# Seven products instead of eight in five units of a pair of merge gates: one more unit in each of three pairs

## The chip, the core and the metric

The kernel runs on one core of a Trainium2 chip. The metric is the device time of one execution in microseconds (us). A core has a matrix engine (TensorE, PE in the profile, with its weight loads as PEld), a vector engine (DVE), a scalar engine (ACT), GpSimd (POOL) and a sync engine (SP) that issues most of the DMA transfers. Each engine takes its instructions in order from a queue of its own and waits at an instruction until what it needs is there.

## The reference

One decoder layer on 256 tokens with a width of 2048, in float32:

```
h = rmsnorm(x, norm_mix_g)
u = h @ w_in                       # split into ten parts
ya = b * causal_dwconv3(c * xa) * silu(za)
yb = rmsnorm(hgrn2(silu(q), f, iv)) * silu(og)
m = sigmoid(ga) * (ya @ w_a) + sigmoid(gb) * (yb @ w_b)
x = x + m @ w_o
x = x + sigmoid(rmsnorm(x) @ w_ple_gate) * (p @ w_ple_proj)
out = rmsnorm(x, final_norm_g)
```

The merge gates ga and gb are the last two parts of u, 2048 columns each. They are what the change is about: `h @ w_in` for 2 x 2048 columns, over a depth of 2048.

## The kernel before

**Products.** Matrices are multiplied in blocks of 128 tokens by 512 columns with a depth of 128. Each float32 operand is split into a high and a low part in a format that TensorE takes at full speed, and a product is three matmuls, high by high, high by low and low by high (`triple`, L1012 to L1014). The token side (`state["hT"]`, xh and xl in the profile) is split once. The weights come from memory all the way through and are split on the fly: ACT copies the high part (whi, L149) and DVE subtracts it from the source to get the low part (wlo, L150). Both are in `cut` and `split`; there are four pairs of whi and wlo buffers.

**Order of the work.** The list `items` holds one entry for each 256 rows of depth by 512 columns of weights. The main loop goes through it and issues, for the item at `pos`: first the combining of the weights of the item at `pos + 2` where that one is of kind S (below), then the split of the item at `pos + 3` (LEAD is 3), then the products of the item itself, then loads further ahead, and then one step of each epilogue that is under way (`advance`). The planner orders TensorE's queue and the DMA queue by its own forecast of when operands are ready. From the gates on, `pinned` fixes the queues of ACT and DVE to the written order.

**Pairs of gates.** Column group j of ga and of gb (512 columns each) form a pair. Pair 0 is multiplied plainly. In pairs 1 to 3 the depth of 2048 falls into eight units of 256 rows. A unit is a product of two by two blocks: two blocks of 128 tokens, two of 128 rows of depth, two of 512 columns. `SEVEN` names the units that are done with seven products instead of eight, by sums and differences of blocks (kind S); the others are kind C, two items of four products. Before, units 0, 2, 4 and 6 are of kind S, so the order is S C C S C C S C C S C C. An S unit needs

- its raw weights, both column groups, in one sraw tile (two buffers);
- the split of the first column group (whi and wlo, L149 and L150), as for any item;
- from `combine_weights` (L164): the split of the block raw[3] (bhi and blo, one buffer), the differences L169, L170 and L171 on DVE in place in sraw, and the split of the four results in two steps (thi and tlo, three buffers);
- sums of token blocks (shi and slo), made once for all pairs by `token_sums` (L715).

`unit_products` (L1039) issues its products in the order of `names_of` (L1029): P1, c00, c10 (into banks s), P5, P7, P6, c01 (into banks g), with the weights whi, whi, bhi, then the halves of thi. P1 and the two c's take the first split, c10 bhi, P5 and P7 the first thi, P6 and c01 the second.

**Banks.** Four accumulation banks are tagged g and four s. A pair takes all eight, g for P6, c01, P5 and P7. Between two pairs the products A (ya by w_a) and B (yb by w_b), four items each, take two banks g each. They are read by DVE: `ep_a` multiplies A into ga (L748), `ep_bb` multiplies B into gb (L760) and adds the two (L764). `ep_bb` is issued at the end of the loop step of the last B item.

**Token sums.** `token_sums` is a generator that moves on by one `yield` at each item after the last one of ga in pair 0. There are 16 items from there to the first S unit. It makes the sums of units 0 and 2, then those of units 4 and 6: each time after four idle steps, the float32 tokens (L726), then in the next step four additions and subtractions (L738) and the split (L740 and L741).

**Memory.** The pool const lasts for the whole kernel, tmp1 until the end of the branches. When `second_part` closes tmp1, the pool st (sraw, bhi, blo, thi, tlo, and the token sums) and tmp2 take its room. The scan's constant `carry` and the masks `near_m` and `full_m` lie in const, and are used only while tmp1 is open.

Of the kernel before, what the change touches and what calls it, by code (L numbers as in the profile page):

```python
# [9 lines left out]
F32 = mybir.dt.float32  # L10
F32R = mybir.dt.float32r
AF = mybir.ActivationFunctionType
ALU = mybir.AluOpType
PSUM = bass.MemoryType.PSUM

P = 128
T = 256
# [11 lines left out]
LB_MAX = 1.0 - 1e-6  # L29
SCAN = 64  # L30
LEVELS = [32, 16, 8, 4]
SEVEN = [(), (0, 2, 4, 6), (0, 2, 4, 6), (0, 2, 4, 6)]
NARROW, Q = len(LEVELS), 32


# [11 lines left out]
def hybrid_kernel(ctx, tc, xT, x, pT, prm, gfin, masks, w_in, w_a, w_b, w_o, w_pg, w_pp, out):  # L47
    nc = tc.nc

    const = ctx.enter_context(tc.tile_pool(name="const", bufs=1))  # L50
# [7 lines left out]
    pools, closers = {}, {}  # L58
# [13 lines left out]
    state = {"tmp": "tmp1"}  # L72
# [3 lines left out]
    def nm(s):  # L76
        uid[0] += 1
        return f"{s}_{uid[0]}"

    def t4(tag="t4", bufs=None):  # L80
        bufs = bufs or {"tmp1": 8, "tmp2": 3, "tmp3": 5}[state["tmp"]]
        return pools[state["tmp"]].tile([P, 1024], F32, tag=tag, bufs=bufs, name=nm(tag))

    def bank(tag):
        return ps.tile([P, CW], F32, tag=tag, bufs=4, name=nm(tag))

    def sc(n, tag="sc", bufs=12):
        return small.tile([P, n], F32, tag=tag, bufs=bufs, name=nm(tag))
# [16 lines left out]
    for gi, (kind, j, w, g, op) in enumerate(groups):  # L105
        if kind == "gb" and SEVEN[j]:
            continue
        for c in range(w.shape[2]):
            it = {"gi": gi, "kind": kind, "j": j, "c": c, "last": c == w.shape[2] - 1}
            if kind != "ga" or not SEVEN[j]:  # L110
                key = ("PP", j // 2) if kind == "PP" else (gi, c // 2)
                items.append(dict(it, w=(w, g, c), raw=key, slot=(j if kind == "PP" else c) % 2))
            elif c in SEVEN[j]:
                items.append(dict(it, kind="S", w=(w, g, c), raw=(gi, c)))
# [6 lines left out]
    def raw_of(pos):  # L121
        it = items[pos]
        if it["raw"] not in loaded:
            if it["kind"] == "S":
                t = pools["st"].tile([P, 2, 2 * CW], F32, tag="sraw", bufs=2, name=nm("sraw"))
            else:
                t = wp.tile([P, 2, 2 * CW], F32, tag="raw", bufs=3, name=nm("raw"))
            loaded[it["raw"]] = t
        return loaded[it["raw"]]
# [15 lines left out]
    def pair_of(pool, n, tags=("whi", "wlo"), width=2 * CW):  # L145
        return tuple(pool.tile([P, width], F32R, tag=tag, bufs=n, name=nm(tag)) for tag in tags)

    def cut(hi, lo, src):
        a = nc.scalar.activation(out=hi, in_=src, func=AF.Copy)  # L149
        v = nc.vector.tensor_tensor(out=lo, in0=src, in1=hi.bitcast(F32), op=ALU.subtract)  # L150
        state["splits"] = (a.ins, v.ins)
# [12 lines left out]
    def combine_weights(pos):  # L164
        st = pools["st"]
        raw = raw_of(pos).rearrange("p n (k c) -> p (n k) c", k=2)
        b22 = pair_of(st, 1, ("bhi", "blo"), CW)
        cut(b22[0], b22[1], raw[:, 3, :])
        nc.vector.tensor_tensor(out=raw[:, 0::2], in0=raw[:, 2:4], in1=raw[:, 0::2], op=ALU.subtract)  # L169
        nc.vector.tensor_tensor(out=raw[:, 3], in0=raw[:, 3], in1=raw[:, 0], op=ALU.subtract)  # L170
        nc.vector.tensor_tensor(out=raw[:, 1], in0=raw[:, 1], in1=raw[:, 3], op=ALU.subtract)  # L171
        ts = []
        for i in range(2):
            hi, lo = pair_of(st, 3, ("thi", "tlo"))
            cut(*(v.rearrange("p (n c) -> p n c", n=2) for v in (hi, lo)), raw[:, i::2])
            ts += [(hi[:, n * CW : (n + 1) * CW], lo[:, n * CW : (n + 1) * CW]) for n in range(2)]
        sums[pos] = (b22, *ts)
# [51 lines left out]
    nc.gpsimd.memset(mhalf, -0.5)  # L229

    nc.scalar.activation(out=sc(8, "table", 1), in_=mhalf, func=AF.Exp)
    carry = const.tile([P, T], F32, name="carry")
    nc.gpsimd.memset(carry, 1.0)
    nc.gpsimd.memset(carry.rearrange("p (n c) -> p n c", c=SCAN)[:, :, 0:1], 0.0)
    near_m = const.tile([P, NARROW, Q], mybir.dt.int32, name="near_m")
    full_m = const.tile([P, 4, P], mybir.dt.int32, name="full_m")
    pw_d = dram.tile([P, 4, 2 * CW], F32, name="pw_d")

    def gain(base, k):
# [475 lines left out]
    def token_sums():  # L715
        nu = len(SEVEN[1])
        state["S"] = pair_of(pools["st"], 1, ("shi", "slo"), nu * 4 * P)
        state["S"] = tuple(v.rearrange("p (u s t) -> p u s t", u=nu, s=4) for v in state["S"])
        for half in range(2):
            for _ in range(4):  # L720
                yield
            F, S = t4(), t4()
            hi, lo = (
                v[:, 8 * half : 8 * half + 8, :].rearrange("p (u r) t -> p u r t", r=4)[:, :, :2] for v in state["hT"]
            )
            nc.vector.tensor_tensor(  # L726
                out=F.rearrange("p (u r t) -> p u r t", u=2, r=2), in0=hi.bitcast(F32), in1=lo.bitcast(F32), op=ALU.add
            )
            yield
            Fv = F.rearrange("p (u r b t) -> p u r b t", u=2, r=2, b=2)  # L730
            Sv = S.rearrange("p (u s t) -> p u s t", u=2, s=4)
            a11, a12, a21, a22 = Fv[:, :, 0, 0], Fv[:, :, 1, 0], Fv[:, :, 0, 1], Fv[:, :, 1, 1]
            s1, s2, s3, s4 = (Sv[:, :, i] for i in range(4))
            for out, u, v, op in (
                (s1, a21, a22, ALU.add), (s2, s1, a11, ALU.subtract),
                (s3, a11, a21, ALU.subtract), (s4, a12, s2, ALU.subtract),
            ):
                nc.vector.tensor_tensor(out=out, in0=u, in1=v, op=op)  # L738
            hi, lo = (v[:, 2 * half : 2 * half + 2] for v in state["S"])
            nc.scalar.activation(out=hi, in_=Sv, func=AF.Copy)  # L740
            nc.vector.tensor_tensor(out=lo, in0=Sv, in1=hi.bitcast(F32), op=ALU.subtract)  # L741
            yield
# [296 lines left out]
    def unit_products(pos):  # L1039
# [3 lines left out]
        def x_of(r, t):  # L1043
            return tuple(v[:, 2 * c + r, t * P : (t + 1) * P] for v in h)
# [8 lines left out]
        b22, t1, t3, t4_, t2 = sums.pop(pos)  # L1053
        s1, s2, s3, s4 = (tuple(v[:, SEVEN[1].index(c), i] for v in state["S"]) for i in range(4))
        for name, op, part in zip(names, (x_of(0, 0), x_of(1, 0), s4, s1, s3, s2, x_of(1, 1)),
# [20 lines left out]
    for pos, it in enumerate(items[:last_group]):  # L1076
        mark = len(nc.cur_bb.bb.instructions)
        kind, j, c, last = (it[n] for n in ("kind", "j", "c", "last"))
        _, _, w, g, opname = groups[it["gi"]]
# [9 lines left out]
        if pos + 2 < len(items) and items[pos + 2]["kind"] == "S":  # L1089
            combine_weights(pos + 2)  # L1090
# [47 lines left out]
        else:  # L1138
            if c == 0:
                psum = [bank("s" if kind == "PP" and j >= 2 else "g") for _ in range(NT)]  # L1140
            hi, lo = parts.pop(pos)
            for i in range(2):
                k = 2 * c + i
                s = slice(i * CW, (i + 1) * CW)
# [10 lines left out]
        if pos == begun:  # L1155
            finish()
            second_part()
            active.append(token_sums())
# [25 lines left out]
    for t, halves in ((0, (0, 1)), (1, (0,)), (1, (1,))):  # L1184
        bk, n = bank("g"), CW // 2
        for c in range(nlast):
# [3 lines left out]
            hi, lo = parts[last_group + c]  # L1190
            for i in range(2):
                k = 2 * c + i
                s = slice(i * CW + halves[0] * n, i * CW + (halves[-1] + 1) * n)
# [83 lines left out]
```

## Time and profile before

| what | value |
|---|---|
| median of 3 runs | 816.61 us (816.34 to 816.72) |
| profiled execution | 817.41 us |
| its span, first to last instruction | 815.6 us |
| TensorE busy | 805.1 us, 99% |
| DVE busy | 592.7 us, 73% |
| ACT busy | 455.0 us, 56% |
| DMA | 186.73 MB, 229 GB/s on average |
| mean granted TensorE clock | 0.996 |

A row of a group gives the line of the code, the engine, the operation, the tiles out<-in, the shapes and the count, then the busy time and the mean duration of one, then the idle time of the engine just before them and what ended it. A row of a timeline gives the start, the duration, the same names and, in brackets, the idle time before it and its releaser. A row of a stage gives the stretch of the span, its length, the busy time and instructions of PE, PEld, DVE, ACT and POOL, the granted clock, the share of the DMA engines and GB/s. Matmuls overlap in their records: the time of one is the distance between two starts.

### The profile page before, as it was taken

How to read it: one execution, taken by the hardware profiler on the slowest of the kernel's cores; microseconds unless marked ns; L12 is line 12 of the kernel's file. 1: busy time of each engine (PE TensorE's matmuls, PEld its weight loads, DVE VectorE, ACT ScalarE, POOL GpSimd, SP SyncE). 2: the span in 40 equal slices, each digit the busy share in tenths (PEclk: the TensorE clock that was granted, in tenths of full speed). 3: DMA queues.
4: the chain of work that ended last, by engine and by line, in shares of the span. 5: the costliest groups of instructions: out<-in, count | busy, mean ns of one | idle time of the engine just before them, and what ended most of it. 6: DMA issues, size and time to landing. Idle time of an engine off the chain costs nothing.

```text
span 815.6 us, 10579 instructions
## 1 busy us (share of the span) xinstructions
PE 805.1 (99%) x4068; PEld 666.2 (82%) x4068; DVE 592.7 (73%) x739; ACT 455.0 (56%) x607; POOL 21.5 (3%) x27
## 2 busy tenths in 40 slices
PE   9999999999999999999999999999999999999995
PEld 6888888888888888888888888888888788888885
DVE  6746588767766498767668988987987756677932
ACT  7576476466565466456445555555545545566623
POOL 1000000001000000010000000000000000001210
PEclk9999999999999999999999999999999999999998
DMA  9988555648767555648774655654744797797702
GB/s 340 392 305 291 194 201 176 232 141 267 249 236 248 201 178 189 209 158 271 266 263 154 232 227 190 233 224 163 275 155 173 265 296 282 250 349 267 274 36 104
DMA packets 46419, 186.73 MB, mean 229 GB/s; under 512 B 6304, under 2 KB 15776, under 8 KB 31648
## 3 DMA queue, kind: packets, MB, share of 16 engines
q1 hardware_dynamic: 45792, 185.00, 64.5%
q10 hardware_dynamic: 576, 1.05, 0.3%
q8 instruction: 32, 0.52, 0.3%
q14 instruction: 19, 0.16, 0.1%
HBM read 172.40 MB, written 13.63 MB: 228 GB/s over the span
## 4 chain that ended last, share of the span: by engine, by line
PE 92%; DVE 2%; issue 2%; DMA 2%; ACT 1%; POOLq 0%; POOL 0%; ACTq 0%
PE g L1013 27%; PE g L1012 27%; PE g L1014 27%; PE s L1013 3%; PE s L1014 3%; PE s L1012 3%; DVE wlo L150 1%; DMA raw<-in_w_pp 1%; DMA raw<-in_w_o 1%; PE s L464 1%; DVE t L288 0%; ACT whi L149 0%; ACT mh L753 0%; PE s L565 0%; PE s L584 0%
## 5 line engine op out<-in xcount | busy, mean ns | idle before, releaser
L150 DVE TENSOR_TENSOR wlo<-raw,whi 128x1024 fp32r<-128x1024 f32 (+1 forms) x270 | 327.5, 1227 | 165.4 <-ACT whi L149 163.4
L149 ACT ACTIVATE whi<-raw 128x1024 fp32r<-128x1024 f32 (+1 forms) x270 | 279.4, 1049 | 214.7 <-PE g L1014 178.1
L1013 PE MATMUL g<-wlo,xh 128*128 128x512 f32 (+1 forms) x744 | 286.1, 384 | 0.0
L1014 PE MATMUL g<-whi,xl 128*128 128x512 f32 (+1 forms) x744 | 285.9, 385 | 0.0
L1012 PE MATMUL g<-whi,xh 128*128 128x512 f32 (+1 forms) x744 | 285.8, 385 | 0.0
L1014 PEld LDWEIGHTS g<-whi,xl 128*128 128x128 f32 x744 | 139.8, 188 | 27.9
L1012 PEld LDWEIGHTS g<-whi,xh 128*128 128x128 f32 x744 | 139.8, 188 | 27.8
L1013 PEld LDWEIGHTS g<-wlo,xh 128*128 128x128 f32 x744 | 139.8, 188 | 27.5
L149 ACT ACTIVATE thi<-sraw 128x1024 fp32r<-128x1024 f32 x24 | 25.5, 1062 | 45.8 <-DVE sraw L169 40.4
L1013 PE MATMUL g<-wlo,mh 128*128 128x512 f32 x128 | 49.9, 390 | 0.3 <-DVE wlo L150 0.3
L1012 PE MATMUL g<-whi,mh 128*128 128x512 f32 x128 | 49.6, 389 | 0.0
L1014 PE MATMUL g<-whi,ml 128*128 128x512 f32 x128 | 49.5, 389 | 0.0
L1012 PE MATMUL s<-whi,xh 128*128 128x512 f32 x96 | 37.3, 389 | 0.0
L1014 PE MATMUL s<-whi,xl 128*128 128x512 f32 x96 | 37.3, 389 | 0.0
L1013 PE MATMUL s<-wlo,xh 128*128 128x512 f32 x96 | 37.3, 389 | 0.0
L150 DVE TENSOR_TENSOR tlo<-sraw,thi 128x1024 fp32r<-128x1024 f32 x24 | 29.3, 1222 | 0.7
L1013 PEld LDWEIGHTS g<-wlo,mh 128*128 128x128 f32 x128 | 24.0, 188 | 5.7 <-DVE wlo L150 0.7
L1012 PEld LDWEIGHTS g<-whi,mh 128*128 128x128 f32 x128 | 24.0, 188 | 5.1
L1014 PEld LDWEIGHTS g<-whi,ml 128*128 128x128 f32 x128 | 24.0, 188 | 4.9
L1012 PE MATMUL g<-whi,yaTh 128*128 128x512 f32 x64 | 24.9, 389 | 0.0
L1013 PE MATMUL g<-wlo,yaTh 128*128 128x512 f32 x64 | 24.9, 389 | 0.0
L1014 PE MATMUL g<-whi,yaTl 128*128 128x512 f32 x64 | 24.9, 389 | 0.0
(208 smaller groups left out, 827.6 us busy)
## 6 DMA issues: line engine op xcount, KB each, us to landing
raw<-in_w_in SPq DMA_DIRECT2D x66, 1024.0 KB, 4.9
raw<-in_w_in SPq DMA_DIRECT2D x34, 512.0 KB, 4.9
raw<-in_w_o SPq DMA_DIRECT2D x16, 1024.0 KB, 6.9
raw<-in_w_pg SPq DMA_DIRECT2D x16, 1024.0 KB, 6.7
sraw<-in_w_in SPq DMA_DIRECT2D x24, 512.0 KB, 4.4
raw<-in_w_a SPq DMA_DIRECT2D x8, 1024.0 KB, 5.6
raw<-in_w_b SPq DMA_DIRECT2D x8, 1024.0 KB, 5.2
turn<-t SPq DMA_DIRECT2D x60, 128.0 KB, 2.7
```

The costliest lines, as they stand in the source:

```text
L149: a = nc.scalar.activation(out=hi, in_=src, func=AF.Copy)
L150: v = nc.vector.tensor_tensor(out=lo, in0=src, in1=hi.bitcast(F32), op=ALU.subtract)
L464: nc.tensor.matmul(out, X[:, 0, h, s], X[:, 1, h, t], start=True, stop=True, tile_position=(0, i * n))
L1012: nc.tensor.matmul(psum, oh, hi, start=first, stop=False)
L1013: nc.tensor.matmul(psum, oh, lo, start=False, stop=False)
L1014: nc.tensor.matmul(psum, ol, hi, start=False, stop=last)
```

## The change

Units 0, 1, 3, 4 and 6 of each of the pairs 1 to 3 are of kind S, where 0, 2, 4 and 6 were. The order of a pair is then S S C C S S C C S C C. The token sums are made in three groups (units 0 and 1, units 3 and 4, unit 6), each after three idle steps instead of four. In `combine_weights`, the first difference (L169) is issued ahead of the split of raw[3]. The three small tiles move from const to tmp1; the token sums grow from four units to five.

```
-SEVEN = [(), (0, 2, 4, 6), (0, 2, 4, 6), (0, 2, 4, 6)]
+SEVEN = [()] + 3 * [(0, 1, 3, 4, 6)]
+TOGETHER = [(0, 2), (2, 2), (4, 1)]
...
         b22 = pair_of(st, 1, ("bhi", "blo"), CW)
+        nc.vector.tensor_tensor(out=raw[:, 0::2], in0=raw[:, 2:4], in1=raw[:, 0::2], op=ALU.subtract)
         cut(b22[0], b22[1], raw[:, 3, :])
-        nc.vector.tensor_tensor(out=raw[:, 0::2], in0=raw[:, 2:4], in1=raw[:, 0::2], op=ALU.subtract)
         nc.vector.tensor_tensor(out=raw[:, 3], in0=raw[:, 3], in1=raw[:, 0], op=ALU.subtract)
...
-    carry = const.tile([P, T], F32, name="carry")
+    carry = pools["tmp1"].tile([P, T], F32, name="carry")
...
-    near_m = const.tile([P, NARROW, Q], mybir.dt.int32, name="near_m")
-    full_m = const.tile([P, 4, P], mybir.dt.int32, name="full_m")
+    near_m = pools["tmp1"].tile([P, NARROW, Q], mybir.dt.int32, name="near_m")
+    full_m = pools["tmp1"].tile([P, 4, P], mybir.dt.int32, name="full_m")
...
-        for half in range(2):
-            for _ in range(4):
+        for first, n in TOGETHER:
+            for _ in range(3):
                 yield
-            F, S = t4(), t4()
+            F, S = (t4()[:, : n * 4 * P] for _ in range(2))
+            c = SEVEN[1][first]
+            hi, lo = (v[:, 2 * c : 2 * (c + n), :] for v in state["hT"])
...
-            hi, lo = (v[:, 2 * half : 2 * half + 2] for v in state["S"])
+            hi, lo = (v[:, first : first + n] for v in state["S"])
```

More of the change, by code (lines that the diff above doesn't have):

```diff
@@ L718, in token_sums @@
         state["S"] = tuple(v.rearrange("p (u s t) -> p u s t", u=nu, s=4) for v in state["S"])
-        for half in range(2):
-            for _ in range(4):
+        for first, n in TOGETHER:
+            for _ in range(3):
                 yield
-            F, S = t4(), t4()
[L723 to L728, printed above, removed]
+            F, S = (t4()[:, : n * 4 * P] for _ in range(2))
+            c = SEVEN[1][first]
+            hi, lo = (v[:, 2 * c : 2 * (c + n), :] for v in state["hT"])
+            Fv = F.rearrange("p (k t) -> p k t", t=T)
+            nc.vector.tensor_tensor(out=Fv, in0=hi.bitcast(F32), in1=lo.bitcast(F32), op=ALU.add)
             yield
-            Fv = F.rearrange("p (u r b t) -> p u r b t", u=2, r=2, b=2)
-            Sv = S.rearrange("p (u s t) -> p u s t", u=2, s=4)
+            Fv = F.rearrange("p (u r b t) -> p u r b t", u=n, r=2, b=2)
+            Sv = S.rearrange("p (u s t) -> p u s t", u=n, s=4)
             a11, a12, a21, a22 = Fv[:, :, 0, 0], Fv[:, :, 1, 0], Fv[:, :, 0, 1], Fv[:, :, 1, 1]
```

## The prediction

> **What bounds the kernel now.** I read the head of the page, then the busy times by stage, the timelines of the vector engine (DVE) and of TensorE around one later pair of gates, and the rows that tell what matrix products wait for.
>
> ```profile
> span 815.6 us, 10579 instructions
> PE 805.1 (99%) x4068; PEld 666.2 (82%) x4068; DVE 592.7 (73%) x739; ACT 455.0 (56%) x607; POOL 21.5 (3%) x27
> ```
>
> TensorE is busy 99% of the span: time leaves only if TensorE gets less to do, and each wait put into it shows in full. But 73% for DVE is an average. By stage (columns: time and busy time of PE, PEld, DVE, ACT, POOL), two later pairs with the stage of A and B products between them:
>
> ```profile
> 506.50:547.30 40.80, 40.80 (x182) 33.78 (x181) 37.73 (x42) 22.19 (x25) 0.00 (x0) 1.00 0.68 245
> 547.30:569.05 21.75, 21.75 (x97) 18.01 (x96) 16.35 (x18) 11.48 (x13) 0.00 (x0) 1.00 0.42 145
> 569.05:609.90 40.85, 40.85 (x182) 33.83 (x181) 37.78 (x42) 22.19 (x25) 0.00 (x0) 1.00 0.61 219
> ```
>
> In a pair TensorE never idles, yet DVE is at 37.7 of 40.8 us: 3.1 us are free in exactly the stage that is changed. In the A/B stage 5.4 us are free, but that helps a pair only as far as DVE may run ahead. How far that is, the timelines tell (start, duration, then in brackets idle time before and its releaser). First ACT, then DVE, then TensorE:
>
> ```profile
> 561.09 1.06 ACT L149 ACTIVATE whi<-sraw 128x1024 fp32r<-128x1024 f32 x1 [1.66 <-PE g L1014]
> ```
>
> ```profile
> 562.18 1.23 DVE L150 TENSOR_TENSOR wlo<-sraw,whi 128x1024 fp32r<-128x1024 f32 x1 [1.49 <-ACT whi L149]
> 563.33 0.68 DVE L150 TENSOR_TENSOR blo<-sraw,bhi 128x512 fp32r<-128x512 f32 x1
> 563.93 1.22 DVE L169 TENSOR_TENSOR sraw<-sraw 128x1024 f32<-128x1024 f32 x1
> 565.18 0.69 DVE L170 TENSOR_TENSOR sraw<-sraw 128x512 f32<-128x512 f32 x1
> 565.90 0.69 DVE L171 TENSOR_TENSOR sraw<-sraw 128x512 f32<-128x512 f32 x1
> 566.51 2.44 DVE L150 TENSOR_TENSOR tlo<-sraw,thi 128x1024 fp32r<-128x1024 f32 x2
> 568.87 2.35 DVE L150 TENSOR_TENSOR wlo<-raw,whi 128x1024 fp32r<-128x1024 f32 x2
> 571.14 1.28 DVE L760 TENSOR_TENSOR gb<-gb,g 128x512 f32<-128x512 f32 x2
> 572.34 1.28 DVE L764 TENSOR_TENSOR t<-ga,gb 128x512 f32<-128x512 f32 x2
> 573.54 1.22 DVE L150 TENSOR_TENSOR wlo<-sraw,whi 128x1024 fp32r<-128x1024 f32 x1
> ```
>
> ```profile
> 569.05 0.39 PE L1012 MATMUL s<-whi,xh 128*128 128x512 f32 x1
> ...
> 609.85 0.39 PE L1012 MATMUL g<-whi,yaTh 128*128 128x512 f32 x1
> ```
>
> The pair starts at 569.05 (call it R) and the next stage at 609.85: 40.80 us for 60 products of three matmuls, so 0.680 us a product (the 0.39 of one matmul overlaps the next). Unit 0's split on DVE begins at 562.18, R - 6.87, and can't sooner: ACT's half of it waited for a product to free one of the four whi buffers, and DVE for ACT. From there DVE is without a gap past 573.54. Starts being 1.14 to 1.25 us apart, I take these slots from the rows: a weight split 1.14; a unit's combining (blo, L169, L170, L171, two tlo) 563.33 to 568.87, 5.54; the two gb products 1.20 and the two additions 1.20.
>
> The order on DVE is the written one (splits of unit 0, its combining, splits of unit 1's two items, then gb, additions, unit 2's split). What the gb products release is shown in the first of the later pairs:
>
> ```profile
> 447.61 1.28 DVE L760 TENSOR_TENSOR gb<-gb,g 128x512 f32<-128x512 f32 x2
> ```
>
> ```profile
> 447.99 0.39 PE L1013 MATMUL s<-wlo,xh 128*128 128x512 f32 x1
> 448.35 0.50 PE L1012 MATMUL g<-thi,shi 128*128 128x512 f32 x1
> ```
>
> ```profile
> L1012 PEld LDWEIGHTS g<-thi,shi 128*128 128x128 f32 x36 | 6.8, 188 | 1.8 <-DVE gb L760 0.4
> ```
>
> Unit 0's last two products (P6 and c01, the last names of names_of) go into the banks that the B product has left only when gb has read them. P6 waited here for gb, and the planner had put a matmul of unit 1 (s<-wlo,xh) ahead of it: TensorE's queue is filled around a late gb, in the order in which operands are due.
>
> **What the change removes.** One more unit of each of three pairs goes from eight products to seven: 3 x 0.680 = **2.04 us less TensorE**, 40.80 - 0.68 = 40.12 us a pair if nothing is late.
>
> **What it adds.** The unit costs DVE one split and one combining, 1.14 + 5.54 = 6.68, in place of two splits, 2.28: +4.40 us a pair. That is more than the 3.1 us free, less 0.68 of a shorter stage. Two such units now stand first (0 and 1, then 3 and 4), so the work is in front. DVE's clock in a pair, from R: unit 0's split at -6.87, its combining from -5.73 to about -0.1 (its steps are only reordered; in the rows none waits), unit 1's split until +1.0, L169 of unit 1 until 2.3. Then blo: its single bhi buffer is read by unit 0's third product, done at 3 x 0.68 + 0.16 = 2.2; ACT's copy is ready at 2.9, so DVE waits 0.65. blo 3.5, L170 4.3, L171 4.9, first tlo 6.1, second 7.3; unit 2's first split 8.4, **gb from 8.4 to 9.6 where it was at 571.14 - 569.05 = 2.1**, additions 10.8, unit 2's second split 12.0, unit 3's 13.1, its combining 18.7, unit 4's split 19.9, first tlo of unit 4 at 19.9 + 1.25 + 0.60 + 0.73 + 0.61 + 1.18 = 24.2. Moving L169 ahead of blo is what keeps that bhi wait at 0.65: behind it, L169 would start at 3.5, 1.25 later.
>
> TensorE: five products of unit 0 until 3.4, three of unit 1 until 5.44, then it needs the first tlo: waits until 6.1, **0.7**. Two products, 7.5; unit 2's first two need its split at 8.45: **1.0**. They end at 9.85 and the gb banks are free. Twenty products stand between there and the fourth of unit 4 (two each that units 0, 1 and 2 still owe, four of unit 2's second item, seven of unit 3, three of unit 4): 9.85 + 13.6 = 23.45, and that tlo comes at 24.25: **0.8**. Behind it unit 5's splits (26.6, 27.7) and unit 6 (33.3 and 34.5) come in time for TensorE at 27.0 and 32.4. Sum 2.5 us of waits, against 0.68 saved: **+1.85 us** in each of pairs 2 and 3.
>
> In the first later pair the third group of token sums falls between the two combinings. The older groups' rows, and unit 0's split in that pair:
>
> ```profile
> L726 DVE TENSOR_TENSOR t<-xh,xl 128x1024 f32<-128x1024 f32 x2 | 2.4, 1218 | 0.0
> L738 DVE TENSOR_TENSOR t<-t,t 128x256 f32<-128x256 f32 x4 | 1.7, 422 | 0.1
> L741 DVE TENSOR_TENSOR slo<-t,shi 128x1024 fp32r<-128x1024 f32 x2 | 2.5, 1226 | 2.3 <-ACT shi L740 2.3
> ```
>
> ```profile
> 438.66 1.22 DVE L150 TENSOR_TENSOR wlo<-sraw,whi 128x1024 fp32r<-128x1024 f32 x1
> ```
>
> This pair starts at 443.68 (447.99, the 20th matmul of it, less 19 x 0.227), so that split stood at R - 5.0, no idle time before it: DVE still made up for the second group. That group now comes two items (5.4 us) sooner, so I let DVE enter at R - 6.87 here too.
>
> Half the width: 0.6 for the sum, 4 subtractions that no row has at 128 columns (between 0.21, half of the row of 256, and 0.42, all of it; I take 0.27, nearer the half), ACT's shi 0.65 waited for, slo 0.6: 3.0 us, of which the 0.65 for bhi is no longer waited: 2.4 on top of the 2.5 of waits, less 0.68: **+4.25** there. If readers of unit 0's sums had to wait for the third group's slo as well (not shown in before, where all sums were done before), its third product would start at 4.1 instead of 1.4, at most 2.7 more.
>
> What else is added has cover. ACT gets 1.5 us more a pair (a combining less one split) and is busy 22.2 of 40.8; while it waits for bhi, only what DVE waits for too is queued behind it. The unit's weights are as many bytes as before. They now go through the two sraw buffers: unit 4's load is issued when unit 1's second tlo is done, at 7.3, and is needed at 18.7; unit 5's, behind it in SP's queue, at 25.5.
>
> ```profile
> DMA to landing us min/median/max: 3.5/4.4/6.5
> ```
>
> ```profile
> PE g L1013 <- DVE wlo L150: 0.3, 1, 0.3
> ```
>
> At 6.5 us the landing leaves 4.9 spare; without that cover each us later would be a us of waiting. Masks and carry only change their place; no instruction is added. No row shows what another address costs, or another tile to wait for; the one place in the trace where TensorE waits for a split lost 0.3 us, so I take 0 and keep 0.3 either way.
>
> Sum: 2 x 1.85 + 4.25 = **+8.0 us**. The profiled execution took 817.41 us (span 815.6 and 1.8 around it), so 825.4 by it; the median of the runs shown, 816.61, is 0.8 below it: **824.6**.
>
> One rule speaks of what such waits do next.
>
> ```profile
> 646.00:648.00 2.00, 2.00 (x11) 1.65 (x10) 0.46 (x1) 1.06 (x1) 0.00 (x0) 1.00 1.00 414
> 648.00:650.00 2.00, 1.73 (x8) 1.13 (x7) 2.00 (x3) 1.10 (x2) 0.00 (x0) 1.00 1.01 426
> ...
> 805.00:810.00 5.00, 2.07 (x18) 1.86 (x16) 1.11 (x4) 1.09 (x4) 0.55 (x1) 0.97 0.00 0
> 810.00:815.60 5.60, 0.00 (x0) 0.00 (x0) 1.04 (x2) 1.23 (x2) 0.00 (x0) 0.50 0.51 187
> ```
>
> A short wait (PE busy 1.73 of 2.00) left the granted clock at 1.00; after the last product it is 0.97 and then 0.50. My waits are 0.7 to 1.9 us long, with products between: I take no loss of clock. The Trainium skill, "TensorE: Matmul & The Clock Gate", Part 1, states that the array falls to half rate after an idle window of about 3.4 us and needs as long in work to come back. By it my sum stays as it is, and the second rival below would cost about 1.7 us more for each of its waits, an estimate from that page.
>
> **The rivals.**
> - *DVE's lead covers it (faster).* If DVE entered each pair 2.5 us earlier (4.9 in the first), nothing waits and only the saving is left: 816.6 - 2.04 = 814.6. It decides at a start of R - 9.4. For it: 5.4 us are free in the A/B stage. Against it: the row at 561.09, where the fourth whi buffer sets the start, and the change adds none. 7%.
> - *TensorE's queue isn't refilled.* If unit 0's P6 keeps its place, all behind it waits for gb: 9.1 - 3.4 = 5.7 us in pairs 2 and 3, 8.1 in the first; 19.5 - 2.04 = +17.5: 834.1. Against it is the row at 447.99. If it holds in some pairs only, each adds 3.2. 10%.
> - *Waits about cancel the saving.* The queue lets products of unit 2 and later stand in for the late ones, waits of 0.7 a pair remain: 816.6. Against it: a split is late too, and no order has anything ready between 7.5 and 8.4. 5%.
>
> **How the numbers follow.** 78% for the forecast, with 821.6 to 828.2 around it: 0.8 x 3, 0.25 and 0.3 less if unit 4's waits vanish, the subtractions take 0.21 each and the moved tiles gain; 2.7, 0.6 and 0.3 more by the bounds above. The range also takes in the second rival in two of the pairs (824.6 + 6.4 = 831) and goes down to 819.5, where unit 2's wait is filled as well (1.0 us) in two pairs; it leaves out the first and third rival and the second in full. A measurement here tells about 0.2% (1.6 us) from no change: faster 0.07, same 0.05 (the third rival), slower 0.88.
>
> **What would show it.** DVE all but gapless in each pair, 0.7 us before a blo of unit 1; gb at R + 8.4 (10.8 in the first pair) instead of 2.1; TensorE waiting in unit 1 for tlo, in unit 2 for wlo, in unit 4 for tlo; pairs of 42.7, 42.7 and 45.1 us. The forecast is wrong if DVE starts a pair well before R - 6.9, if gb comes before unit 1's combining, or if P6 stands ahead of unit 1's products in TensorE's queue.

## The result, and the profile after

The changed kernel takes 827.39 us (median of 4 runs, 826.60 to 828.46), the kernel before 816.64 (816.34 to 816.72): a ratio of 1.0133, 95% interval 1.0116 to 1.0151. It is **slower by 10.8 us**; the forecast was 8.0 us, with 819.5 to 831.0 as its range. The profiled execution took 828.46 us. The head of its page:

```profile
span 826.1 us, 10577 instructions
PE 808.8 (98%) x4059; PEld 665.8 (81%) x4059; DVE 607.7 (74%) x760; ACT 459.4 (56%) x614; POOL 22.4 (3%) x27
```

TensorE has nine matmuls less, the three products that were to go, and yet is longer at work and less densely. Where, the starts of the matmuls tell. I divide the span at the first matmul of each pair, at the first one of the A products behind it, and at the first one of the last matrix (PG). All other stretches are equal in both profiles (the stages between the pairs 21.76, PG to the last matmul 87.55).

| stretch | before | after | difference | forecast |
|---|---|---|---|---|
| up to the first pair | 443.68 | 444.39 | +0.71 | 0 |
| pair 1 | 41.05 | 45.08 | +4.03 | +4.25 |
| pair 2 | 40.80 | 42.78 | +1.98 | +1.85 |
| pair 3 | 40.80 | 42.79 | +1.99 | +1.85 |
| from A of pair 3 to PG | 109.39 | 111.27 | +1.88 | 0 |
| sum | | | +10.59 | +7.95 |

The stages of the second and third pair (time, then the busy time of PE, PEld, DVE and ACT), with the A/B stage between them:

```profile
511.23:554.01 42.78, 41.14 (x178) 32.92 (x177) 41.49 (x46) 21.49 (x24) 0.00 (x0) 1.00 0.66 217
554.01:575.77 21.76, 21.76 (x97) 18.03 (x96) 16.85 (x20) 13.16 (x15) 0.00 (x0) 1.00 0.50 179
575.77:618.56 42.79, 41.13 (x178) 32.92 (x177) 41.51 (x46) 21.48 (x24) 0.00 (x0) 1.00 0.58 196
```

Before, TensorE was busy for all of a pair and DVE had 3.1 us to spare. Now DVE is busy for 41.5 of 42.8 us and TensorE is the one that stands still. DVE's timeline of pair 3, whose start R is 575.77. The lines of the code have moved: the split is L150 and L151 here, the second and third difference of a combining L171 and L172, the gb products L759, the additions L763:

```profile
568.91 1.23 DVE L151 TENSOR_TENSOR wlo<-sraw,whi 128x1024 fp32r<-128x1024 f32 x1 [1.30 <-ACT whi L150]
570.17 1.23 DVE L169 TENSOR_TENSOR sraw<-sraw 128x1024 f32<-128x1024 f32 x1
571.31 0.69 DVE L151 TENSOR_TENSOR blo<-sraw,bhi 128x512 fp32r<-128x512 f32 x1
572.03 0.69 DVE L171 TENSOR_TENSOR sraw<-sraw 128x512 f32<-128x512 f32 x1
...
575.72 1.22 DVE L151 TENSOR_TENSOR wlo<-sraw,whi 128x1024 fp32r<-128x1024 f32 x1
576.98 1.22 DVE L169 TENSOR_TENSOR sraw<-sraw 128x1024 f32<-128x1024 f32 x1
578.73 0.69 DVE L151 TENSOR_TENSOR blo<-sraw,bhi 128x512 fp32r<-128x512 f32 x1 [0.53 <-ACT bhi L150]
...
583.22 1.22 DVE L151 TENSOR_TENSOR wlo<-raw,whi 128x1024 fp32r<-128x1024 f32 x1
584.36 1.28 DVE L759 TENSOR_TENSOR gb<-gb,g 128x512 f32<-128x512 f32 x2
...
599.22 2.51 DVE L151 TENSOR_TENSOR tlo<-sraw,thi 128x1024 fp32r<-128x1024 f32 x2
```

DVE enters at R - 6.86 as before, runs without a gap but for 0.53 us at unit 1's blo, and comes to gb at R + 8.59. TensorE in the same pair (x2 is two matmuls in one row, the second 0.23 behind the first):

```profile
581.22 0.61 PE L1011 MATMUL g<-thi,shi 128*128 128x512 f32 x2
582.06 0.50 PE L1012 MATMUL g<-tlo,shi 128*128 128x512 f32 x1 [0.23 <-DVE tlo L151]
583.09 0.46 PE L1011 MATMUL s<-whi,xh 128*128 128x512 f32 x1
584.00 0.50 PE L1011 MATMUL s<-whi,xh 128*128 128x512 f32 x1 [0.44 <-ACT whi L150]
...
598.92 0.61 PE L1011 MATMUL g<-thi,shi 128*128 128x512 f32 x2
600.52 0.50 PE L1011 MATMUL g<-thi,shi 128*128 128x512 f32 x1 [0.99 <-ACT thi L150]
```

It waits in three places: in unit 1 for the first tlo (the start is 0.4 later than 0.227 behind the matmul before it), in unit 2 for its split (0.7), in unit 4 for thi and tlo (1.1). Behind each of the three the next matmul too starts 0.34 later instead of 0.227, 0.1 each. The bracket counts from the end of the matmul before, so it shows less than what is lost. Products of unit 1 and two of unit 2 stand ahead of unit 0's P6: the queue was filled around the late gb.

### The profile page after: what moved, and what is told of

It is laid out like the page before. It is cut to its first block, busy times and chain, and to the rows that moved or that the text cites. A ratio compares the mean times of both kernels' runs of the same rounds, so it can differ in the third digit from the quotient of the medians.

```text
span 826.1 us, 10577 instructions
## 1 busy us (share of the span) xinstructions
PE 808.8 (98%) x4059; PEld 665.8 (81%) x4059; DVE 607.7 (74%) x760; ACT 459.4 (56%) x614; POOL 22.4 (3%) x27
## 3 DMA queue, kind: packets, MB, share of 16 engines
q10 hardware_dynamic: 576, 1.05, 0.3%
## 4 chain that ended last, share of the span: by engine, by line
PE 83%; DVE 8%; issue 4%; ACT 3%; DMA 1%; POOLq 0%; POOL 0%; ACTq 0%; DVEq 0%
PE g L1011 25%; PE g L1012 25%; PE g L1013 25%; DVE wlo L151 3%; PE s L1011 2%; PE s L1012 2%; PE s L1013 2%; ACT thi L150 1%; DVE sraw L169 1%; ACT whi L150 1%; DMA raw<-in_w_o 1%; DVE sraw L171 1%; DVE sraw L172 1%; DVE blo L151 1%; PE s L465 1%
## 5 line engine op out<-in xcount | busy, mean ns | idle before, releaser
L151 DVE TENSOR_TENSOR wlo<-raw,whi 128x1024 fp32r<-128x1024 f32 (+1 forms) x264 | 320.0, 1228 | 159.0 <-ACT whi L150 157.4
L150 ACT ACTIVATE whi<-raw 128x1024 fp32r<-128x1024 f32 (+1 forms) x264 | 272.4, 1049 | 206.5 <-PE g L1013 168.8
L150 ACT ACTIVATE thi<-sraw 128x1024 fp32r<-128x1024 f32 x30 | 31.8, 1061 | 52.2 <-DVE sraw L169 36.1
L151 DVE TENSOR_TENSOR tlo<-sraw,thi 128x1024 fp32r<-128x1024 f32 x30 | 36.6, 1222 | 0.8
L1011 PE MATMUL s<-whi,xh 128*128 128x512 f32 x84 | 33.5, 405 | 1.3 <-ACT whi L150 1.3
L1012 PE MATMUL s<-wlo,xh 128*128 128x512 f32 x84 | 33.0, 393 | 0.0
L1013 PE MATMUL s<-whi,xl 128*128 128x512 f32 x84 | 32.9, 392 | 0.0
L1012 PE MATMUL g<-wlo,ybTh 128*128 128x512 f32 x64 | 25.0, 391 | 0.6 <-DVE wlo L151 0.6
L1013 PE MATMUL g<-whi,ybTl 128*128 128x512 f32 x64 | 24.9, 389 | 0.0
```

Of the source, the lines that this page charges most:

```text
L1011: nc.tensor.matmul(psum, oh, hi, start=first, stop=False)
L1012: nc.tensor.matmul(psum, oh, lo, start=False, stop=False)
L1013: nc.tensor.matmul(psum, ol, hi, start=False, stop=last)
```

## The experiments

My theory: DVE has too much work in a pair, and most of it in front, so its results come late. Rivals: the banks (gb comes late, whatever DVE's work), the moved tiles, and the place of the units rather than their number. The two stretches that the forecast lacked, ahead of the first pair and behind the last, were open as well. Each kernel is timed against the kernel before on the same chip, whose medians were 816.57, 817.57 and 816.78 us in the three groups of runs (816.64 for the changed kernel), so ratios are compared.

| kernel | median us | ratio to before (95%) | pairs 1, 2, 3 (us) | A of pair 3 to PG |
|---|---|---|---|---|
| changed kernel | 827.39 | 1.0133 (1.0116 to 1.0151) | 45.08, 42.78, 42.79 | 111.27 |
| masks_alone | 816.86 | 1.0003 (0.9994 to 1.0012) | 41.07, 40.80, 40.80 | 108.80 |
| sums_early | 825.03 | 1.0102 (1.0085 to 1.0118) | 42.80, 42.79, 42.78 | 111.58 |
| gb_first | 826.38 | 1.0121 (1.0106 to 1.0136) | 44.90, 42.33, 42.10 | 111.70 |
| subs_out | 817.02 | 1.0003 (0.9993 to 1.0012) | 41.72, 40.44, 40.41 | 109.05 |
| old_order | 829.08 | 1.0142 (1.0127 to 1.0157) | 44.64, 43.68, 43.70 | 110.74 |
| spread | 823.31 | 1.0070 (1.0053 to 1.0087) | 42.61, 41.27, 41.30 | 112.05 |
| best | 831.80 | 1.0179 (1.0161 to 1.0196) | 45.95, 45.24, 44.51 | 110.96 |
| pair3_three | 823.97 | 1.0082 (1.0066 to 1.0097) | 44.90, 42.80, 41.48 | 108.86 |
| spread_subs_out | 816.43 | 0.9995 (0.9985 to 1.0004) | 40.44, 40.12, 40.12 | 109.99 |
| spread_pool | 824.50 | 1.0092 (1.0075 to 1.0109) | 43.20, 41.85, 41.91 | 111.43 |

**The moved tiles alone** (edit against the kernel before):

```
-    carry = const.tile([P, T], F32, name="carry")
+    carry = pools["tmp1"].tile([P, T], F32, name="carry")
...
-    near_m = const.tile(...)
-    full_m = const.tile(...)
+    near_m = pools["tmp1"].tile(...)
+    full_m = pools["tmp1"].tile(...)
```

> The kernel before, with carry, near_m and full_m taken from tmp1 instead of const and nothing else. If the work of the vector engine is the cause, 816.6 us within 0.5, and every pair 40.8 us long. If the moved tiles (other addresses, other tiles to wait for) cost what the pairs don't explain (0.7 us before the first pair and 1.9 us behind the last in the profiled execution of after), 817.3 to 819.2.

Ratio 1.0003, with 1 in its interval, and pairs of the same length. That rival is out.

**The token sums four items earlier:**

```
-            for _ in range(3):
+            for _ in range(2):
```

> The changed kernel with two idle steps instead of three ahead of each group of token sums, so that the third group is done four items before the first pair. If DVE's work in front of a pair is the cause, the first pair shrinks from 45.1 us to the 42.8 of the other two, the time falls by 2.3 us to about 825.1, and the half-clock stretch of the first pair (454 to 458 us) goes with it. If the token sums don't matter and the first pair is longer for another reason (the clock), it stays at 45 us and the time at 827.4.

The first pair is 42.80 us, like the others. 2.3 us of the first pair were the third group of sums, as DVE's clock had it. The half-clock stretch of the first pair, shown in the section on the prediction, is gone too; but two runs below that keep the sums where they were (gb_first and old_order) don't have it either, so its going isn't shown to be the work of the sums.

**gb ahead of the second combining:**

```
+        late = kind == "B" and last and j < 3
+        if not late:
+            front(pos)
...
                 step(active[-1])
+            if late:
+                front(pos)
```

Here `front` is the combining of the item at `pos + 2` and the split of the one at `pos + 3`.

> The changed kernel, but in the loop step of the last B item the combining of unit 1 and the split of unit 2's first item are issued behind the products and ep_bb, so gb is read at about R + 1.2 instead of R + 8.5. If the late release of the two banks by gb is what costs (the rival), P6 and c01 come in place, the pairs fall to 40.1 us plus what the token sums take, and the time to about 817 us. If it is DVE's amount of work, the wait only moves: unit 1's combining now stands behind gb and the additions, TensorE waits about 1.3 us for unit 1's tlo and 1.1 for unit 4's, the pairs are 42.5 us and the time falls by 0.5 to 1.5 us, to about 826.4.

This tells the banks from the work. DVE's timeline of pair 3, with gb back at R + 1.1:

```profile
574.16 1.22 DVE L151 TENSOR_TENSOR wlo<-sraw,whi 128x1024 fp32r<-128x1024 f32 x1
575.30 1.28 DVE L759 TENSOR_TENSOR gb<-gb,g 128x512 f32<-128x512 f32 x2
576.49 1.29 DVE L763 TENSOR_TENSOR t<-ga,gb 128x512 f32<-128x512 f32 x2
577.70 1.22 DVE L169 TENSOR_TENSOR sraw<-sraw 128x1024 f32<-128x1024 f32 x1
```

What TensorE waits for in that kernel (microseconds in total, times, longest):

```profile
PE g L1011 <- ACT thi L150: 5.1, 6, 1.4
```

Only 0.2, 0.45 and 0.7 us are won in the three pairs. The wait in unit 2 is gone and the one in unit 4 has stayed. The one in unit 1 has moved from tlo to thi, and in pairs 2 and 3 it has grown (the row counts unit 1's and unit 4's, two in a pair): unit 1's combining, L169 the first of it, now starts at R + 3.5 instead of 1.2, behind the two gb products and the two additions. The banks that gb frees are not what sets the length of a pair; they were only the next thing in DVE's queue. In the whole time the intervals of this run and of the changed kernel overlap.

**Two of the four differences left out** (the weights of two of four blocks stay uncombined):

```
-        nc.vector.tensor_tensor(out=raw[:, 3], in0=raw[:, 3], in1=raw[:, 0], op=ALU.subtract)
-        nc.vector.tensor_tensor(out=raw[:, 1], in0=raw[:, 1], in1=raw[:, 3], op=ALU.subtract)
```

> The changed kernel without the two half-width differences of combine_weights (L171 and L172): the weights of five units are left uncombined in two of four blocks, and DVE has 1.33 us less per unit, 6.7 us less per pair; all else, gb's place in the order too, is as it was. If DVE's work is the cause, pairs 2 and 3 fall to about 40.9 us and the first to 42.7, DVE is no longer behind at the end of the third, and the time is 827.4 - 1.9 x 2 - 2.3 - 1.9 = 819 or a little less. If gb's place is the cause, P6 still waits until R + 7.4 and the pairs keep 42 us or more: 824 to 826.

More than expected came back: 817.02 us where I gave 819, nearly all that the change had cost. Pairs 2 and 3 by stage:

```profile
507.24:547.68 40.44, 40.44 (x178) 33.17 (x177) 35.80 (x38) 22.95 (x27) 0.00 (x0) 1.00 0.73 244
569.44:609.85 40.41, 40.41 (x178) 33.16 (x177) 35.77 (x38) 22.83 (x27) 0.00 (x0) 1.00 0.62 220
```

DVE is at 35.8 instead of 41.5 us, TensorE loses 0.3 us a pair instead of 2.7 (its products alone take 40.12), and the stage behind pair 3 is at 109.05. gb stood where it stands in the changed kernel, behind unit 1's combining. This kernel leaves DVE with less work than it had before the change (37.7), so it shows that DVE's work is the cause, not how little of it would do.

**L169 behind blo again:**

```
+        cut(b22[0], b22[1], raw[:, 3, :])
         nc.vector.tensor_tensor(out=raw[:, 0::2], in0=raw[:, 2:4], in1=raw[:, 0::2], op=ALU.subtract)
-        cut(b22[0], b22[1], raw[:, 3, :])
```

> The changed kernel with L169 put back behind the split of raw[3], as before. If DVE's single queue in front of the pair is the cause, L169 of unit 1 now waits with blo for the bhi buffer: pairs 2 and 3 grow by 0.9 to 1.25 us each, to 43.7 to 44.0, the first (where the token sums cover that wait) by nothing or less than 0.5, and the time is 829.2 to 830. If the reordering itself costs (blo next to L171 starts 0.12 later than blo next to L169), undoing it wins 0.1 us per unit: 826 to 827.

Pairs 2 and 3 are 0.9 longer. The first is 0.4 shorter, where up to 0.5 longer was expected; it keeps the full clock, which explains 0.2 of that at most (see the first pair below), and the rest is open. The wait that the reordering avoids, in DVE's timeline of pair 3:

```profile
575.20 1.22 DVE L151 TENSOR_TENSOR wlo<-sraw,whi 128x1024 fp32r<-128x1024 f32 x1
578.33 0.69 DVE L151 TENSOR_TENSOR blo<-sraw,bhi 128x512 fp32r<-128x512 f32 x1 [1.91 <-ACT bhi L150]
```

1.91 us instead of 0.53, with L169 still to do. In the whole time it shows less clearly: 1.0142 against 1.0133, with intervals that overlap.

**Other units, the same number:**

```
-SEVEN = [()] + 3 * [(0, 1, 3, 4, 6)]
-TOGETHER = [(0, 2), (2, 2), (4, 1)]
+SEVEN = [()] + 3 * [(0, 2, 3, 5, 6)]
+TOGETHER = [(0, 1), (1, 2), (3, 2)]
...
-            for _ in range(3):
+            for _ in range(3 if first == 0 else 1):
```

> Five units in each pair as in the changed kernel, but units 0, 2, 3, 5 and 6 instead of 0, 1, 3, 4 and 6 (unit 1 is plain, so gb comes before the second combining), with token sums of units 0, then 2 and 3, then 5 and 6, the later groups after one idle step. The same work on every engine. If where DVE's work stands is what costs, the pairs fall to about 41.4 us (waits of 0.25 in unit 3 and 1.05 in unit 6 against 0.68 saved), and with DVE still late behind the third pair the time is 816.6 + 3 x 0.6 + 1.9 = 820.3. If the amount of work alone decides, the place changes nothing: 825 (as with early sums).

The place counts for 1.5 us in each of pairs 2 and 3: 41.3 as expected. The time does not come down to the ratio that 820.3 would be (1.0045; measured 1.0070): the first pair is at 42.6 and the stage behind the third at 112.05, 2.7 over before. So five units cost more than they save in both of the places tried: 41.3 against 40.8.

**Less work for DVE, some of it for GpSimd** (on top of the last one; the second thi and tlo of a unit are also issued behind the next split, an edit of the main loop that is not printed here):

```
-        nc.vector.tensor_tensor(out=raw[:, 1], in0=raw[:, 1], in1=raw[:, 3], op=ALU.subtract)
+        nc.gpsimd.tensor_tensor(out=raw[:, 1], in0=raw[:, 1], in1=raw[:, 3], op=ALU.subtract)
...
-            nc.vector.tensor_tensor(out=spread(m, t), ..., op=ALU.add)
+            (nc.vector if j == 3 else nc.gpsimd).tensor_tensor(out=spread(m, t), ..., op=ALU.add)
```

> As the run with units 0, 2, 3, 5 and 6, and with less work on DVE: the additions of ep_bb (L763) for pairs 0 to 2 and the last difference (L172) of each unit go to GpSimd, and the second thi and tlo are issued behind the next split, to cover GpSimd's time. DVE has 1.2 + 5 x 0.61 = 4.25 us less per pair, about what the fifth unit added. If DVE's work is the cause of all that was lost, the pairs are 40.2 to 40.6 us and the stage behind them 109.4 again: 814.7 to 816.2, faster than both. If GpSimd is slower than twice DVE (its 1.27 us for 128x512 in the gfin products) or the two engines slow one another, tlo comes later and the time is 817 to 822.

This was to beat both kernels and is the slowest of all, 831.80 us. DVE and GpSimd in pair 2:

```profile
508.09 1.22 DVE L151 TENSOR_TENSOR tlo<-sraw,thi 128x1024 fp32r<-128x1024 f32 x1
509.23 2.31 DVE L151 TENSOR_TENSOR wlo<-raw,whi 128x1024 fp32r<-128x1024 f32 x1
```

```profile
508.40 2.06 POOL L172 TENSOR_TENSOR sraw<-sraw 128x512 f32<-128x512 f32 x1 [28.04 <-DVE sraw L171]
```

GpSimd starts at 508.40 and is done at 510.46. A split on DVE that takes 1.22 us alone takes 2.31 beside it and ends 1.1 us after GpSimd is done, as if it began then. To spare DVE 0.61 us cost it 1.1. The pairs are 3.2 to 4.0 us longer than in the run before this one. How much of that comes from GpSimd and how much from the later thi and tlo, this run doesn't tell; the next one has only the additions on GpSimd.

**GpSimd for the additions only:**

```
-            nc.vector.tensor_tensor(out=spread(m, t), ..., op=ALU.add)
+            (nc.vector if j == 3 else nc.gpsimd).tensor_tensor(out=spread(m, t), ..., op=ALU.add)
```

> The run with units 0, 2, 3, 5 and 6, with the additions of ep_bb (L763) of pairs 0 to 2 on GpSimd and nothing else moved: DVE has 1.2 us less per pair, GpSimd two operations of 1.3 to 2.1 us each. If the engines run side by side, the waits in unit 6 shrink by 1.2 us, the pairs are 40.6 us and the time 2.5 to 4 us under that of the run without. If DVE's own operations are held up while GpSimd works (in the run with more on GpSimd a split beside it took 2.31 us instead of 1.22), the 3.5 us of GpSimd cost DVE about 1.7 us for the 1.2 it is spared: pairs 0.3 to 0.6 us longer, 1 to 2 us slower.

Pairs 0.6 us longer, as if the engines exclude one another. GpSimd's additions, then DVE's split and its neighbour beside them:

```profile
511.48 3.52 POOL L763 TENSOR_TENSOR t<-ga,gb 128x512 f32<-128x512 f32 x2 [60.04 <-DVE gb L759]
```

```profile
511.91 1.94 DVE L151 TENSOR_TENSOR wlo<-sraw,whi 128x1024 fp32r<-128x1024 f32 x1
513.88 2.20 DVE L169 TENSOR_TENSOR sraw<-sraw 128x1024 f32<-128x1024 f32 x1
```

1.94 and 2.20 for what takes 1.22 and 1.23: 1.7 us lost for 1.2 spared.

**Three units in the last pair:**

```
-SEVEN = [()] + 3 * [(0, 1, 3, 4, 6)]
+SEVEN = [()] + 2 * [(0, 1, 3, 4, 6)] + [(0, 3, 6)]
```

> The changed kernel with five units in pairs 1 and 2, and three (0, 3 and 6) in pair 3. TensorE has two products more, 1.36 us, in pair 3 than in the changed kernel. If DVE's backlog at the end of the third pair is what costs 1.9 us in the stage behind it (transposes and splits of m), that stage is back at about 109.4 us, pair 3 takes 61 products, 41.5 us instead of 42.8, and the time is 827.4 - 1.3 - 1.9 = 824.2. If that stage is longer for another reason (another order of TensorE's queue, other tiles to wait for), only 1.3 us go: 826.1.

Pair 3 takes 41.48 us, its 61 products and no wait, and the stage behind it is at 108.86. So DVE's backlog at the end of pair 3 is what that stage paid for. The other kernels bear it out. Where the gates' last operations on DVE start 1.05 to 1.1 us behind the first A product (before, masks_alone and this one), the stage takes 108.8 to 109.4 us; at 1.8 us (subs_out) 109.05, at 2.5 (spread_subs_out) 110.0, at 3.4 to 3.6 (best, old_order, gb_first, the changed kernel, sums_early) 110.75 to 111.7, at 4.4 and 4.5 (spread_pool, spread) 111.4 and 112.05.

**Other units and two differences less:** the edits of the run with other units and of the run with two differences left out, together (two of four blocks stay uncombined).

> The run with units 0, 2, 3, 5 and 6, without the two half-width differences L171 and L172 (the weights of two of four blocks stay uncombined), so DVE has 6.7 us less per pair. If DVE's work is all that hid the saving, nothing waits: pairs 2 and 3 take their 59 products, 40.1 to 40.2 us, the first at most 40.6, the stage behind them 109.4 or less: 2.0 us under the kernel before, ratio 0.9975. If something else in five units costs TensorE time (banks, weight loads, the queue's order), the pairs stay at 40.4 or more, as in the changed kernel without those differences.

The second pair by stage:

```profile
505.60:545.72 40.12, 40.12 (x178) 33.22 (x177) 35.84 (x38) 21.25 (x25) 0.00 (x0) 1.00 0.68 240
```

The saving exists in full, 0.68 us a pair, once DVE has 5.7 us less to do. The time shows less of it: 0.9995 (0.9985 to 1.0004), not told from no change, where I gave 0.9975. Most of the rest is lost behind the third pair, where I had expected 109.4 or less: DVE still comes out of the pair late, and the stage takes 109.99. Against masks_alone, whose pairs are those of the kernel before and whose stage takes 108.80, the pairs win 2.0 and the stage loses 1.2; the last matmul starts 0.8 sooner (805.14 against 805.96). The medians show 0.35 of these 0.8; the remaining 0.5 is open.

## Why the prediction was right, and where it was short

- **The saving.** 2.04 us: nine matmuls less, and pairs of 40.12 us when nothing waits. Right.
- **DVE's clock** (when DVE comes to each of its operations). Entry at R - 6.87, measured -6.86; 0.65 us at bhi, measured 0.53; gb at 8.4, measured 8.59, and in the first pair 10.8, measured 10.68 (455.07 - 444.39). The third group's subtractions and split, with the wait for ACT between them, took 2.3 us as worked out. One slot was short: a unit's split and combining take 575.72 - 568.91 = 6.81 in the new order, where I took 1.14 + 5.54 = 6.68. In the rows, L169 follows the split by 1.26, not 1.14, and L171 follows blo by 0.72, not 0.60; 0.1 of that comes back, as blo follows L169 by 1.14 where L170 had followed it by 1.25. So "its steps are only reordered" cost 0.1 a unit, and TensorE went on in unit 4 at R + 24.75, where I had 24.25.
- **TensorE's waits.** In the three places named, 0.4, 0.7 and 1.1 instead of 0.7, 1.0 and 0.8, and 0.1 behind each, which the forecast lacked. The sum of a pair, 1.98, is close to the forecast's 1.85 (1.82 by its own terms), in part by luck: unit 4 went on 0.5 later than worked out, but the queue had 98 matmuls in front of that place where I counted 96, as two matmuls with thi had moved ahead of the wait for tlo, and these are worth 0.45. Both named rivals fell: the queue was refilled, and the lead stayed at 6.86.
- **The first pair.** 45.08 us for the 45.1 that was written; the difference is 4.03 and not 4.25 because the first pair of before took 41.05, not the 40.80 that I started from. It didn't come about in the way that was written. "I take no loss of clock" was wrong there. TensorE's row for the late tlo and three of those behind it:

```profile
452.77 0.50 PE L1012 MATMUL g<-tlo,shi 128*128 128x512 f32 x1 [1.36 <-DVE tlo L151]
...
455.73 0.63 PE L1012 MATMUL s<-wlo,xh 128*128 128x512 f32 x1
456.15 0.63 PE L1013 MATMUL s<-whi,xl 128*128 128x512 f32 x1
456.58 0.63 PE L1011 MATMUL s<-whi,xh 128*128 128x512 f32 x1
```

and the stretches around them, where the third number from the end is the granted clock:

```profile
449.00:454.00 5.00, 2.99 (x12) 1.57 (x10) 4.86 (x7) 3.36 (x4) 0.00 (x0) 1.00 0.04 15
454.00:459.00 5.00, 4.56 (x13) 3.44 (x13) 5.00 (x8) 2.12 (x3) 0.00 (x0) 0.66 0.76 232
```

  Starts are 0.42 us apart instead of 0.227, for some 3.4 us: about 1.4 us of work lost, after a stretch in which TensorE was busy for 2.99 of 5.00 us and no wait was over 1.8 us long. It hardly added to the sum, since DVE sets the end of the pair: TensorE came to unit 4 later and had nothing left to wait for there. The run pair3_three has the same code up to its third pair; its clock fell 1.9 us sooner in the first pair, it still waited in unit 4, and the pair took 44.90. So the lost clock cost 0.2 us here. In the run with early sums neither is there, and the pair is shorter by the 2.3 us of DVE's work.

  The Trainium skill, "TensorE: Matmul & The Clock Gate", Part 1, ties the drop to an idle window of about 3.4 us; the section "A second HAM failure mode: psum-queue depth-cycling" of the same page says that frequent short idling between groups of matmuls can swing the gate as well. This case is nearer to the second: 0.66, with no wait over 1.8 us. What decides it no run here shows: in gb_first TensorE was busy for 2.42 of 5.00 us in the same place (449.30 to 454.30), in old_order for 2.94 (447.10 to 452.10), and both kept a granted clock of 1.00 in the pair.
- **What was missing.** The step that failed is the **sum**: it ended with the third pair and had no term for what is behind it. The gates' last operations on DVE, before and after, against the first A product (609.85 and 618.56):

```profile
610.90 1.28 DVE L681 TENSOR_TENSOR gb<-gb,s 128x512 f32<-128x512 f32 x2
```

```profile
622.16 1.28 DVE L682 TENSOR_TENSOR gb<-gb,s 128x512 f32<-128x512 f32 x2
```

  1.05 us behind it before, 3.60 after: DVE leaves the third pair 2.5 us later. Behind pairs 1 and 2 this costs nothing, the A/B stage takes 21.76 us in both kernels. Behind pair 3 DVE also turns and splits m, between the splits of the weights, and TensorE waits for these. Its waits in that stage of the changed kernel:

```profile
639.23 0.50 PE L1012 MATMUL g<-wlo,ybTh 128*128 128x512 f32 x1 [0.56 <-DVE wlo L151]
...
658.17 0.73 PE L1011 MATMUL g<-whi,mh 128*128 128x512 f32 x2 [0.49 <-ACT whi L150]
659.43 0.50 PE L1012 MATMUL g<-wlo,mh 128*128 128x512 f32 x1 [0.53 <-DVE wlo L151]
```

  Before there was one such wait, of 0.3 us in its bracket. It is 1.88 us in all, and the run with three units in the last pair takes it away. The profile of masks_alone, whose code is the same there, has no such wait and a stage of 108.80, so the wait of before isn't in every execution; against 108.80 the stage costs 2.5.
- **The 0.71 us ahead of the first pair** are none of the change's. In this execution the first products ran at the lower rate: from 5.7 to 7.4 us their starts are 0.43 us apart, and between 4 and 8 us from the start it has 11 matmuls where the one of before has 16 (the column of the clock shows 1.00 for both; the starts tell):

```profile
4.00:8.00 4.00, 3.94 (x11) 2.42 (x10) 3.10 (x6) 3.11 (x6) 0.00 (x0) 1.00 0.95 341
```

```profile
4.00:8.00 4.00, 3.87 (x16) 2.42 (x14) 2.78 (x6) 2.99 (x6) 0.00 (x0) 1.00 0.97 335
```

  With the same code at the start, eight of the ten other kernels' profiles begin their first pair between 443.4 and 443.8 us, one at 443.1, one at 444.2. Without it, 8.0 in the pairs and 1.9 behind them make 9.9 of the 10.8 us. If most executions of before lack its one wait, as its median, 0.8 under its profiled execution, suggests, the stage costs 2.5 and the sum is 10.5.

## What to carry to other kernels

An algorithm that saves products pays on the engine that prepares operands: compare what it adds there with what that engine has free **in that stage**, not with its share of the whole span (73% was 92% here). Then follow that engine's queue from the point where its lead is set, and go on behind the changed stage until it has caught up; a backlog is paid for wherever the next stage has no room. Where work stands in the queue was worth 1.5 us a pair here, but moving one late operation ahead of another (gb) won 0.2 to 0.7, because the sum of the work was the limit.

## What the runs showed of the hardware that I had not expected

- A two-operand operation of GpSimd holds up DVE's: a split of 1.22 us took 2.31 beside 2.06 us of GpSimd, and 3.5 us of GpSimd cost DVE 1.7 us. The Trainium skill, "SBUF — State Buffer", section "SBUF: two separate sides", says that a GpSimd operation that reads SBUF and a DVE operation with two inputs in SBUF lock one another out for a whole instruction; these rows agree.
- On DVE, an operation that changes in place what the one just before it had read started 0.11 to 0.12 us later than otherwise: L169 1.26 behind the split, L171 0.72 behind blo, against 1.15 and 0.60 for blo behind the split and L169 behind blo in the old order. One that reads what the one before it has just written is as late: L170 behind L169 1.25 in the old order, against 1.14 for blo behind L169 in the new.
- The granted clock fell to 0.66 over 5 us after a stretch with TensorE 60% busy, without any single wait over 1.8 us. A stretch with 48% (gb_first) left it at 1.00, so the busy share of 5 us alone doesn't decide.
